# HGRN scan on one Trainium2 core: a level's four row multiplications made as two, with a stepped access pattern

## The chip, the core and the metric

One core of a Trainium2 chip runs the whole program. The metric is device microseconds of one execution; lower is better. Engines: TensorE (PE; its weight loads are listed as PEld), the Vector engine (DVE), ScalarE (ACT), GpSimd (POOL) and SyncE (SP).

## The reference, cut to what matters

One step of a two-layer diffusion backbone over 128 context and 512 latent tokens (T = 640 together). Each layer has one input projection, three bidirectional scans (SSD, HGRN2, mLSTM), a gated merge and a feed-forward part. The change is in the HGRN2 scan, four heads per layer, each in both directions:

```python
def hgrn_scan(q, k, v, logf, s0):
    causal = jnp.tril(jnp.ones((H_CHUNK, H_CHUNK), dtype=bool))[..., None]
    def step(s, inp):
        qc, kc, vc, gc = inp
        g = jnp.cumsum(gc, axis=-2)
        diff = jnp.where(causal, g[..., :, None, :] - g[..., None, :, :], 0.0)
        w = jnp.exp(diff) * causal
        att = jnp.einsum("bhtk,bhsk,bhtsk->bhts", qc, kc, w)
        o = jnp.einsum("bhts,bhsv->bhtv", att, vc) + jnp.einsum("bhtk,bhkv->bhtv", qc * jnp.exp(g), s)
        ...
```

A query at t and a key at s < t meet through the product of all forget gates f between them, channel by channel.

## The kernel before, in words

**Stages.** A layer runs bulk work on TensorE (projections of 128 rows by 640 tokens, with split weights: three matmuls of 320 columns for each half and each block of 128 inputs) and, woven into it, the scans. `drive` does this: a scan is a generator that yields numbers, and for each unit yielded one quantum of bulk work is emitted, which for a projection is six matmuls (`accumulate`, L485 to L494). TensorE's order is the order in which the code emits. Vector engine, ScalarE, SP and GpSimd are ordered by the build's scheduler, statically; each engine then works its own list in order, waiting on semaphores.

**A head of the HGRN scan** (`hgrn_scan`, L1258). The tile QK holds four sections of T columns: section 0 is q for the backward direction, 1 and 2 the keys k of forward and backward, 3 is q forward. Instead of a product over chunks, seven levels work on blocks of L = 1, 2, 4, ..., 64 tokens. At a level, pairs of neighbouring blocks of L meet: ScalarE copies the keys of both directions, a half of each pair of blocks from section 1 and the other half from section 2, into `hk` (L1293); TensorE multiplies them with the matching halves of sections 0 and 3 into the PSUM tiles `hl`, in two groups of three and two chunks of 128 (L1305); two COPY_PREDICATED put those scores that belong to this level into A (`hA`, L1323). Then the keys and queries must be carried to the block size 2L: half of the blocks of each section are multiplied by the product of the gates of the neighbouring block, which stands in the tile F (views `Fs[li]`, two sections of T/L values). These are the four multiplications of the change, L1316 to L1321, in the order of sections 1, 2, 0, 3. Below, sections 1 and 2 are the inner ones, 0 and 3 the outer ones. L1324 makes the next level's gate products.

So a level's `hk` needs the inner sections after the level before, and its `hl` needs `hk` and the outer sections. Between the `hl` of two levels the scan yields 3, which is 18 bulk matmuls.

**Beside it on the Vector engine**: the low parts of split weights (`wl`, L412), row products for the modulation (`jk`, `wa`, L289, with a small `mod`, L294). **On ScalarE**: the high parts of split weights (`wh`, L411) and copies of finished projections (`hq`, `mq`, `hth`, `val`, `bgt`). SP's queue issues the loads of weights.

Of the kernel before, what the change touches and what calls it, by code (L numbers as in the profile page):

```python
# [12 lines left out]
ALU = mybir.AluOpType  # L13
# [3 lines left out]
P = 128  # L17
# [4 lines left out]
T = CTX + SMP  # L22
# [86 lines left out]
def backbone(ctx, tc, a):  # L109
    nc = tc.nc  # L110
    pe, act, dve, pool_e = nc.tensor, nc.scalar, nc.vector, nc.gpsimd
# [16 lines left out]
    def ut(s, dt=F32):  # L128
        return up.tile([P, UW], dt, name=nm(s), tag="u")
# [4 lines left out]
    def bank(s):  # L134
        return ps.tile([P, 512], F32, name=nm(s), tag="ps")
# [612 lines left out]
    def mixers(i, h, ssum, spill, starter, spill_x, first_tickets):  # L748
# [5 lines left out]
        def qt(s):  # L754
            return qp.tile([P, 2560], F32, name=nm(s), tag="q")
# [482 lines left out]
        def halves_of(base, gap, L, nb):  # L1238
            return bass.AP(base.tensor, base.offset, [list(base.ap[0]), [2 * L, nb], [gap + L, 2], [1, L]])
# [18 lines left out]
        def hgrn_scan(u, hd):  # L1258
            q = u["q"]
            QK = qt("QK").rearrange("p (s f) -> p s f", s=4)  # L1260
# [10 lines left out]
            for d in range(2):  # L1271
# [3 lines left out]
                    out=f, in0=u[f"f{d}"][:, :T], scalar1=fsc[:, i, col], scalar2=fbi[:, i, col], op0=ALU.mult, op1=ALU.add  # L1275
# [14 lines left out]
            for li, L in enumerate(LEVELS):  # L1290
                nb = T // (2 * L)
                kk = ut("hk")
                act.activation(  # L1293
                    out=kk[:, :T].rearrange("p (b h j) -> p b h j", h=2, j=L), in_=halves_of(QK[:, 1, :], T, L, nb), func=AF.Copy
                )
                if li:
                    yield 3
                else:
                    yield 1
                copies = []  # L1300
                for c0, c1 in groups:
                    pt = bank("hl")
                    for c in range(c0, c1):
                        sl = slice(c * P, (c + 1) * P)
                        pe.matmul(  # L1305
                            pt[:, (c - c0) * P : (c - c0 + 1) * P], kk[:, sl], halves_of(QK[:, 0, sl], 3 * T, L, P // (2 * L)),
                            start=True, stop=True,
                        )
                    copies.append(dict(
                        out=A[:, c0 * P : c1 * P].rearrange("p (c f) -> p c f", f=P),  # L1310
                        mask=lmask[:, li, :].unsqueeze(1).to_broadcast([P, c1 - c0, P]),
                        data=pt[:, : (c1 - c0) * P].rearrange("p (c f) -> p c f", f=P),
                    ))
                fv = Fs[li].rearrange("p s (b h) -> p s b h", h=2)
                qv = QK.rearrange("p s (b h j) -> p s b h j", h=2, j=L)
                for s_ in (1, 2, 0, 3):  # L1316
                    half, s2 = s_ // 2, s_ % 2
                    dst = qv[:, s_, :, half, :]
                    dve.tensor_tensor(
                        out=dst, in0=dst, in1=fv[:, s2, :, 1 - half].unsqueeze(2).to_broadcast([P, nb, L]), op=ALU.mult,  # L1320
                    )  # L1321
                for cp in copies:
                    dve.copy_predicated(**cp)  # L1323
                dve.tensor_tensor(out=Fs[li + 1], in0=fv[:, :, :, 0], in1=fv[:, :, :, 1], op=ALU.mult)  # L1324
# [11 lines left out]
            for n in range(4):  # L1336
                pt = bank("hup")
                for d in range(2):
                    j = 2 * n + d
# [6 lines left out]
                for d in range(2):  # L1346
                    c = order[2 * n + d][1]
                    dve.scalar_tensor_tensor(
                        out=Sv[:, n, d, :], in0=Sv[:, n - 1, d, :], scalar=Fl[:, 1 - d, c : c + 1],
                        in1=pt[:, d * P : (d + 1) * P], op0=ALU.mult, op1=ALU.add,  # L1350
# [115 lines left out]
        def bg_item(f):  # L1466
# [7 lines left out]
            return item(f"bg{f}", O_BG + f * P, "bg", done)  # L1474

        kinds = (("S", ssd_items, sz_items, ssd_scan), ("H", hgrn_items, hg_item, hgrn_scan), ("M", mlstm_items, mo_item, mlstm_scan))
        of_kind = {k_: [{} for _ in range(4)] for k_ in "SHM"}
        units = [(k_, n, of_kind[k_][n]) + tuple(fs) for k_, *fs in kinds for n in range(4)]
# [162 lines left out]
    h, staged = modulator(0, x, 1, staged=True)  # L1641
# [141 lines left out]
    for i in range(DEPTH):  # L1783
# [13 lines left out]
        with tc.tile_pool(name=f"ff{i}", bufs=NF) as fp:  # L1797
# [37 lines left out]
            blocks, half, twin_blocks = block_modulator(i, x, fp)  # L1835
            h = [tuple(tuple(blocks[k][hf][:, m * HALF : (m + 1) * HALF] for hf in range(2)) for m in range(2)) for k in range(KT)]
# [4 lines left out]
            for n_, (p0, p1) in enumerate(PARTS):  # L1841
# [58 lines left out]
                if i + 1 < DEPTH:  # L1900
                    ada_need(i + 1, 15)
                    h, half = modulator(i + 1, x, 1)
                else:
                    half = final
# [107 lines left out]
```

## Time and profile before

| | |
|---|---|
| three runs | 2805.67, 2806.61, 2809.32 us, median 2806.61 |
| the profiled execution | 2810.28 us, of which the span of the trace is 2808.5 |
| TensorE, matmuls | 2755.0 us busy (98%) |
| Vector engine | 1914.2 us (68%), 3854 instructions |
| ScalarE | 1230.1 us (44%) |
| granted TensorE clock, mean | 0.993 of full |
| chain that ended last | TensorE 92%, Vector engine 3% |
| the four multiplications, L1319 | 224 of 128x320, 97.6 us busy |

Busy time of an engine is the time in which it had an instruction in work; on the Vector engine neighbouring instructions overlap by a little, so the sum of durations is larger than the busy time, and the time from start to start is shorter than a duration. In a timeline, a row's first number is its start in us from the start of the span, the second the time from the first start to the last end of the merged instructions, xN their number; a bracket gives idle time before it and what ended it.

### The profile page before, as it was taken

To read this page: it belongs to the slowest core of one execution; us is meant where nothing else is said; L and a number is where in the kernel's file an instruction comes from. 1 tells how busy PE (TensorE), PEld (TensorE's weight loads), DVE (VectorE), ACT (ScalarE), POOL (GpSimd) and SP (SyncE) were. 2 spreads that over 40 slices of the span, in tenths; PEclk is the share of its full clock that TensorE was granted. 3 is DMA by queue.
4 is the path that set the end of the run, shared out by engine and by line. 5 is a ranking of instruction groups with operands and counts; after the bars stand their busy time and mean duration, and the time that the engine had idled before them with its cause. 6 is when DMAs were issued, how large, how long until landed. Compare 5 with 4: busy or idle time off the path is not lost.

```text
span 2808.5 us, 48685 instructions
## 1 busy us (share of the span) xinstructions
PE 2755.0 (98%) x19262; PEld 2704.8 (96%) x19262; DVE 1914.2 (68%) x3854; ACT 1230.1 (44%) x2436; POOL 280.3 (10%) x474
## 2 busy tenths in 40 slices
PE   7999999999899999999999999999999999999998
PEld 6999999999899999999999999999999999999998
DVE  6657678777555586777777665888765556747475
ACT  5545434445442363342455544344445225425243
POOL 0111100000031100000001211000101200000000
PEclk9999999999999999999999999999999999999999
DMA  8444423434364324344534444333433733333433
GB/s 315 130 114 137 122 93 123 126 130 121 127 239 162 103 64 153 125 127 166 172 100 126 125 122 137 116 113 128 124 123 132 254 105 96 100 130 103 130 108 98
DMA packets 119300, 373.43 MB, mean 133 GB/s; under 512 B 16072, under 2 KB 28688, under 8 KB 118944
## 3 DMA queue, kind: packets, MB, share of 16 engines
q1 hardware_dynamic: 92720, 269.56, 30.7%
q0 software_dynamic: 26352, 100.76, 10.5%
q8 instruction: 152, 2.49, 0.4%
q14 instruction: 76, 0.62, 0.1%
HBM read 316.04 MB, written 54.21 MB: 132 GB/s over the span
## 4 chain that ended last, share of the span: by engine, by line
PE 92%; DVE 3%; DMA 2%; ACT 2%; issue 1%; SPq 0%; POOL 0%; ACTq 0%; DVEq 0%; POOLq 0%
PE ga L422 17%; PE ab L494 15%; PE bg L494 12%; PE br L494 8%; PE hfp L494 4%; PE sz L494 4%; PE xT L494 4%; PE hl L1305 2%; PE ga L494 2%; PE hgp L494 2%; PE hqp L494 2%; PE mkp L494 2%; PE BT L494 2%; PE CT L494 2%; PE mop L494 1%; PE val L1042 1%
## 5 line engine op out<-in xcount | busy, mean ns | idle before, releaser
L411 ACT ACTIVATE wh<-wr 128x1024 fp32r<-128x1024 f32 (+3 forms) x354 | 351.5, 996 | 569.0 <-PE br L494 144.1
L412 DVE TENSOR_TENSOR wl<-wr,wh 128x1024 fp32r<-128x1024 f32 (+3 forms) x354 | 407.7, 1153 | 191.2 <-ACT wh L411 186.6
L422 PE MATMUL ga<-hb,wh 128*128 128x320 f32 x912 | 201.6, 308 | 0.0
L1561 DVE SCALAR_TENSOR_TENSOR x<-ab,hg,x 128x128 f32<-128x128 f32 (+2 forms) x192 | 73.2, 433 | 170.3 <-PE ab L494 170.3
L494 PE MATMUL bg<-hh,wh 128*128 128x320 f32 x768 | 188.0, 326 | 0.0
L422 PE MATMUL ga<-hth,wl 128*128 128x320 f32 x608 | 187.8, 309 | 0.0
L422 PE MATMUL ga<-htl,wh 128*128 128x320 f32 x608 | 187.8, 309 | 0.0
L422 PE MATMUL ga<-hth,wh 128*128 128x320 f32 x608 | 187.7, 309 | 0.0
L494 PE MATMUL bg<-hl,wh 128*128 128x320 f32 x768 | 175.4, 310 | 0.0
L494 PE MATMUL bg<-hh,wl 128*128 128x320 f32 x768 | 175.2, 309 | 0.0
L494 PE MATMUL ab<-uh,wh 128*128 128x320 f32 x704 | 164.8, 310 | 0.0
L494 PE MATMUL ab<-ul,wh 128*128 128x320 f32 x704 | 164.1, 309 | 0.0
L494 PE MATMUL ab<-uh,wl 128*128 128x320 f32 x704 | 164.1, 309 | 0.0
L422 PEld LDWEIGHTS ga<-hb,wh 128*128 128x128 f32 x912 | 152.4, 188 | 0.0
L422 PE MATMUL ga<-hb,wl 128*128 128x320 f32 x456 | 140.6, 308 | 0.0
L494 PEld LDWEIGHTS bg<-hl,wh 128*128 128x128 f32 x768 | 129.3, 189 | 0.0
L494 PEld LDWEIGHTS bg<-hh,wh 128*128 128x128 f32 x768 | 127.0, 190 | 2.1 <-issue 0.8
L494 PEld LDWEIGHTS bg<-hh,wl 128*128 128x128 f32 x768 | 128.9, 189 | 0.0
L494 PEld LDWEIGHTS ab<-ul,wh 128*128 128x128 f32 x704 | 118.8, 188 | 0.2
L494 PEld LDWEIGHTS ab<-uh,wh 128*128 128x128 f32 x704 | 118.7, 188 | 0.2
L494 PEld LDWEIGHTS ab<-uh,wl 128*128 128x128 f32 x704 | 118.7, 188 | 0.0
L1153 ACT ACTIVATE E<-E,gsb 128x128 f32<-128x128 f32 x320 | 99.6, 392 | 37.3 <-POOL E L943 37.3
(497 smaller groups left out, 7552.7 us busy)
## 6 DMA issues: line engine op xcount, KB each, us to landing
wr<-w_in SPq DMA_DIRECT2D x152, 512.0 KB, 3.5
wr<-w_gu SPq DMA_DIRECT2D x88, 512.0 KB, 3.7
wa<-w_ada SPq DMA_DIRECT2D x84, 512.0 KB, 3.6
E<-rows_s SPq DMA_DIRECT2D x80, 256.0 KB, 5.8
x<-xd POOLq DMA_DIRECT2D x64, 320.0 KB, 3.7
wr<-w_down SPq DMA_DIRECT2D x32, 512.0 KB, 4.1
sp<-bgt POOLq DMA_DIRECT2D x48, 320.0 KB, 3.5
bgr<-sp POOLq DMA_DIRECT2D x48, 320.0 KB, 4.9
```

The source lines that it names most:

```text
L411: act.activation(out=hi[:, :n], in_=raw[:, :n], func=AF.Copy)
L412: dve.tensor_tensor(out=lo[:, :n], in0=raw[:, :n], in1=hi[:, :n].bitcast(F32), op=ALU.subtract)
L422: pe.matmul(bank_[:, :HALF], a_[:, sl], b_, start=first and j == m == 0, stop=j == n - 1 and m == 2, skip_group_check=True,)
L494: pe.matmul(out[hf][:, :HALF], wt_[:, sl], b_, start=m == k == 0, stop=m == 2 and k == n - 1)
L1042: pe.matmul(o, xh[:, sl], hi[:, wsl], start=k == 0, stop=False)
L1153: act.activation(out=e[:, j * P : (j + 1) * P], in_=e[:, j * P : (j + 1) * P], func=AF.Exp, bias=gv["sb"][:, d, c, 4 * g + j : 4 * g + j + 1],
L1305: pe.matmul(pt[:, (c - c0) * P : (c - c0 + 1) * P], kk[:, sl], halves_of(QK[:, 0, sl], 3 * T, L, P // (2 * L)), start=True, stop=True,)
L1561: dve.scalar_tensor_tensor(out=x_[:, lo:hi], in0=pt[:, lo - hf * HALF : hi - hf * HALF], scalar=gate[:, 2 * f + j : 2 * f + j + 1], in1=x_ ...
```

## The change

Per level, the multiplications of sections 1 and 2 become one operation over `2 x nb x L` elements (nb = T/2L), and those of 0 and 3 another. The access pattern of the destination steps from one section's blocks to the other's by T + L, or by 3T + L; that of the factor steps back or forward between the two sections of F.

```diff
                 fv = Fs[li].rearrange("p s (b h) -> p s b h", h=2)
-                qv = QK.rearrange("p s (b h j) -> p s b h j", h=2, j=L)
-                for s_ in (1, 2, 0, 3):
-                    half, s2 = s_ // 2, s_ % 2
-                    dst = qv[:, s_, :, half, :]
-                    dve.tensor_tensor(
-                        out=dst, in0=dst, in1=fv[:, s2, :, 1 - half].unsqueeze(2).to_broadcast([P, nb, L]), op=ALU.mult,
-                    )
+                for q0, step, f0, back in ((T, T + L, 2 * nb + 1, -2 * nb - 1), (0, 3 * T + L, 1, 2 * nb - 1)):
+                    dst = bass.AP(QK.tensor, QK.offset + q0, [list(QK.ap[0]), [step, 2], [2 * L, nb], [1, L]])
+                    by = bass.AP(fv.tensor, fv.offset + f0, [list(fv.ap[0]), [back, 2], [2, nb], [0, L]])
+                    dve.tensor_tensor(out=dst, in0=dst, in1=by, op=ALU.mult)
                 for cp in copies:
                     dve.copy_predicated(**cp)
```

TensorE's and GpSimd's orders stay as they were. On the Vector engine, ScalarE and SP instructions move, all within the HGRN stages. Names in the rows: out<-in with tile names, the size, and in brackets the engines' semaphores that the instruction waits for.

The Vector engine in the first head, level 2 (blocks of 4) and the start of level 3; before:

```order
L1319 TENSOR_TENSOR QK_4325<-QK_4325,F_4326 128x80x4 [waits Activation_49]
L1319 TENSOR_TENSOR QK_4325<-QK_4325,F_4326 128x80x4 [waits DVE_49]
L1319 TENSOR_TENSOR QK_4325<-QK_4325,F_4326 128x80x4 [waits DVE_49,PE_49]
L1319 TENSOR_TENSOR QK_4325<-QK_4325,F_4326 128x80x4 [waits DVE_49]
L1323 COPY_PREDICATED hA_4335<-lmask,hl_4477 128x384 [waits DVE_49]
L1323 COPY_PREDICATED hA_4335<-lmask,hl_4481 128x256 [waits DVE_49]
L1319 TENSOR_TENSOR QK_4325<-QK_4325,F_4326 128x40x8 [waits Activation_49]
```

and of the change, where L1318 is the merged multiplication and L1320 the predicated copy:

```order
L1320 COPY_PREDICATED hA_4335<-lmask,hl_4473 128x384 [waits DVE_49,PE_49]
L1318 TENSOR_TENSOR QK_4325<-QK_4325,F_4326 128x2x80x4 [waits PE_49,Activation_49]
L1320 COPY_PREDICATED hA_4335<-lmask,hl_4477 128x256 [waits DVE_49]
L1318 TENSOR_TENSOR QK_4325<-QK_4325,F_4326 128x2x80x4 [waits DVE_49]
L294 TENSOR_SCALAR mod_86<-mod_86,pv_84 128x2
L1320 COPY_PREDICATED hA_4335<-lmask,hl_4505 128x384 [waits PE_49]
L1318 TENSOR_TENSOR QK_4325<-QK_4325,F_4326 128x2x40x8 [waits PE_49,Activation_49]
```

The inner multiplication now waits for TensorE too, and stands behind the first predicated copy; the outer stands behind the second one, and waits for the inner.

TensorE at the products `hl` of the same level, with a bulk matmul on either side; before:

```order
L494 MATMUL hqp_4424<-hh_397,wl_4359 128x320
L1305 MATMUL hl_4477<-QK_4325,hk_4451 128x128 [waits DVE_49,PE_49,Activation_49]
L1305 MATMUL hl_4477<-QK_4325,hk_4451 128x128 x2
L1305 MATMUL hl_4481<-QK_4325,hk_4451 128x128 [waits PE_49]
L1305 MATMUL hl_4481<-QK_4325,hk_4451 128x128
L494 MATMUL hqp_4423<-hh_404,wh_4358 128x320
```

and of the change:

```order
L494 MATMUL hqp_4422<-hh_397,wl_4359 128x320
L1305 MATMUL hl_4473<-QK_4325,hk_4447 128x128 [waits PE_49,Activation_49]
L1305 MATMUL hl_4473<-QK_4325,hk_4447 128x128 x2
L1305 MATMUL hl_4477<-QK_4325,hk_4447 128x128 [waits PE_49]
L1305 MATMUL hl_4477<-QK_4325,hk_4447 128x128
L494 MATMUL hqp_4421<-hh_404,wh_4358 128x320
```

The place is the same; the wait for the Vector engine is gone from the first product, and in the built program the count for which ScalarE's `hk` waits is now that of the outer multiplication (it was that of the second inner one).

ScalarE in the second head, from the copy of level 0 to that of level 2; before:

```order
L1293 ACTIVATE hk_4997<-QK_4923 128x640 [waits DVE_49]
L1288 ACTIVATE hA_4933<-hd_4993 128x256 [waits PE_49]
L1293 ACTIVATE hk_5019<-QK_4923 128x640 [waits DVE_49]
L411 ACTIVATE wh_5342<-wr_5139 128x1024 [waits DMAHW2_49,PE_49]
L959 ACTIVATE hq_5033<-hqp_4946 128x320 [waits DMASW3_49,PE_49]
L959 ACTIVATE hq_5033<-hqp_4947 128x320 [waits PE_49]
L1293 ACTIVATE hk_5063<-QK_4923 128x640 [waits DVE_49]
```

and of the change:

```order
L1293 ACTIVATE hk_4983<-QK_4909 128x640 [waits DVE_49]
L1288 ACTIVATE hA_4919<-hd_4979 128x256 [waits PE_49]
L411 ACTIVATE wh_5314<-wr_5117 128x1024 [waits DMAHW2_49,PE_49]
L1293 ACTIVATE hk_5003<-QK_4909 128x640 [waits DVE_49]
L959 ACTIVATE hq_5017<-hqp_4932 128x320 [waits DMASW3_49,PE_49]
L959 ACTIVATE hq_5017<-hqp_4933 128x320 [waits PE_49]
L1293 ACTIVATE hk_5045<-QK_4909 128x640 [waits DVE_49]
```

The weight split `wh` has moved ahead of the copy of level 1; the fourth head has the same move.

## Rows read from the trace of the kernel before

**Rows 1.** Busy time by engine in the HGRN stages of both layers: us, busy (xcount), PEclk.

```profile
380.00:620.00 240.00, 239.31 (x1786) 237.52 (x1785) 195.90 (x423) 102.51 (x211) 11.88 (x22) 1.00 0.36 117
1760.00:2000.00 240.00, 239.22 (x1784) 237.12 (x1783) 201.18 (x432) 101.99 (x209) 11.87 (x22) 1.00 0.36 119
```

**Rows 2.** Line L1305: what ended the idle time before it (us, times).

```profile
  ACT hk L1293: 4.9, 16
```

**Rows 3.** Timeline of PEld, head 0: the loads of `hl`, levels 0, 1, 2, 4.

```profile
403.10 1.60 PEld L1305 LDWEIGHTS hl<-QK,hk 128*128 128x128 f32 x10 [0.43 <-ACT hk L1293]
407.52 1.26 PEld L1305 LDWEIGHTS hl<-QK,hk 128*128 128x128 f32 x10
411.32 1.23 PEld L1305 LDWEIGHTS hl<-QK,hk 128*128 128x128 f32 x10
...
418.86 1.23 PEld L1305 LDWEIGHTS hl<-QK,hk 128*128 128x128 f32 x10
```

**Rows 4.** The same for heads 1 (levels 0, 4, 5), 2 and 3 (levels 0, 4).

```profile
460.70 1.60 PEld L1305 LDWEIGHTS hl<-QK,hk 128*128 128x128 f32 x10 [0.44 <-ACT hk L1293]
...
474.66 1.20 PEld L1305 LDWEIGHTS hl<-QK,hk 128*128 128x128 f32 x10
477.90 1.20 PEld L1305 LDWEIGHTS hl<-QK,hk 128*128 128x128 f32 x10
...
520.06 1.60 PEld L1305 LDWEIGHTS hl<-QK,hk 128*128 128x128 f32 x10 [0.44 <-ACT hk L1293]
...
535.75 1.22 PEld L1305 LDWEIGHTS hl<-QK,hk 128*128 128x128 f32 x10
...
577.59 1.60 PEld L1305 LDWEIGHTS hl<-QK,hk 128*128 128x128 f32 x10 [0.43 <-ACT hk L1293]
...
592.87 1.20 PEld L1305 LDWEIGHTS hl<-QK,hk 128*128 128x128 f32 x10
```

**Rows 5.** Tile QK: its multiplications of 320 and 640 elements, ns min/median/max.

```profile
L1319 DVE TENSOR_TENSOR QK<-QK,F x224: 462/483/495, 405.1 to 1983.7; 128x320 f32<-128x320 f32 x112
...
L1278 DVE TENSOR_TENSOR QK<-hq,F x16: 815/818/821, 385.2 to 1945.7; 128x640 f32<-128x640 f32 x16
```

**Rows 6.** Timeline of the Vector engine: one of 640 elements and the next instruction.

```profile
385.19 0.82 DVE L1278 TENSOR_TENSOR QK<-hq,F 128x640 f32<-128x640 f32 x1
385.93 0.48 DVE L1199 TENSOR_TENSOR yt<-yt,ytr 128x128 f32<-128x128 f32 x2
```

**Rows 7.** Timelines of Vector engine and ScalarE, head 0, from level 0 to level 1.

```profile
405.10 1.70 DVE L1319 TENSOR_TENSOR QK<-QK,F 128x320 f32<-128x320 f32 x4
406.72 0.44 DVE L1323 COPY_PREDICATED hA<-lmask,hl 128x256 f32<-128x256 uint8 x1
407.05 1.21 DVE L412 TENSOR_TENSOR wl<-wr,wh 128x1024 fp32r<-128x1024 f32 x1
...
406.66 0.81 ACT L1293 ACTIVATE hk<-QK 128x640 f32<-128x640 f32 x1
```

**Rows 8.** The same two engines in head 0, levels 2 to 4.

```profile
411.74 0.89 DVE L1319 TENSOR_TENSOR QK<-QK,F 128x320 f32<-128x320 f32 x2
412.77 0.89 DVE L1319 TENSOR_TENSOR QK<-QK,F 128x320 f32<-128x320 f32 x2 [0.15 <-PE hl L1305]
...
416.34 0.60 DVE L1323 COPY_PREDICATED hA<-lmask,hl 128x384 f32<-128x384 uint8 x1
416.83 0.88 DVE L1319 TENSOR_TENSOR QK<-QK,F 128x320 f32<-128x320 f32 x2
...
412.71 0.74 ACT L1293 ACTIVATE hk<-QK 128x640 f32<-128x640 f32 x1 [1.73 <-DVE QK L1319]
```

**Rows 9.** Timeline of ScalarE, head 1: the weight split near level 1.

```profile
464.38 1.05 ACT L411 ACTIVATE wh<-wr 128x1024 fp32r<-128x1024 f32 x1
```

**Rows 10.** TensorE in the next scan: us, busy (xcount), PEclk, DMA share, GB/s.

```profile
705.00:710.00 5.00, 1.68 (x11) 1.00 0.70 266
710.00:715.00 5.00, 5.00 (x27) 0.66 0.00 0
```

## The prediction

> **What bounds the kernel now.** First the busy times of the two HGRN stages, by stretch [rows 1]: in 240 us TensorE works 239.3, in the second layer 239.2; the Vector engine works 196 and 201. So TensorE is the bound in both, and the Vector engine has a sixth of its time to spare. Second, what TensorE waited for before a level's product hl [rows 2]: 4.9 us over 16 waits in 56 levels. Eight of these are the first level of a head, 0.43 or 0.44 each, 3.5 in all [rows 3, 4]; the change does not touch them. What is left, 1.4 us, is all that shortening the multiplications can give back directly. Third, the pace of the levels, as the starts of TensorE's loads for hl [rows 3, 4]: TensorE does five products for hl, then 18 bulk matmuls of a projection, and the levels follow each other every 3.8 us in head 0 and every 3.2 us in head 1. So nothing of the scan holds TensorE today: the copy hk and the multiplications of a level run beside the bulk matmuls. The question is how much room they have there.
>
> **The change, part by part.** Names: level 0 to 6 of a head; "inner" are sections 1 and 2 of QK, which the next copy hk reads; "outer" are sections 0 and 3, which the products hl read.
>
> (a) Work of the Vector engine. 224 multiplications of 320 elements become 112 of 640: 0.483 and 0.818 us [rows 5]. Back to back, one is issued every 0.41 us (four in 1.70 [rows 7]), one of 640 every 0.74 (385.19 to 385.93 [rows 6]). Each merge frees 2 x 0.41 - 0.74 = 0.07 us, 112 of them 8 us. The row for 640 is of contiguous rows; the 320 ones already step through memory at every level, and all take 0.462 to 0.495, so I take no extra for the pattern. These 8 us lie beside TensorE's work [rows 1]; I cost them at nothing. Bounds: 0 to -1.4 us.
>
> The Trainium skill, "VectorE: DVE Perf Modes", section "Rules for kernel authors", says of chained operations to keep down their number, not the semaphores. By that rule the change is a gain, of the 8 us worked out in (a) at most. The trace says that the engine that would gain is not the one that bounds.
>
> (b) The order of the scan. A merged operation reaches over all that lies between its two rows: the inner pair over sections 1 and 2, the outer pair over 0 to 3, sections 1 and 2 included. The build orders accesses to QK by this reach, wherever it doesn't see that they are apart. So three waits come in, seen in the order above: at levels 0 to 3 the inner operation waits for the products hl of its own level (before: from level 2 on for hk alone); the outer waits for the inner; and the next copy hk waits for the outer. The last shows on TensorE: hl names no wait for the Vector engine any more, as hk has already waited for the later operation. Besides, one COPY_PREDICATED stands between inner and outer. Before, the inner operations of a level could run while TensorE was at hl, and hk of the next level began before or beside the outer ones. Now it is one chain: hl, inner, predicated copy, outer, hk, next hl.
>
> Its length, from the start of hl:
> - To the Vector engine's start after all five products: 405.10 - 403.10 = 2.00 us at level 0 [rows 3, 7], 412.77 - 411.32 = 1.45 later [rows 3, 8]. At levels 2 and 3 the first predicated copy fits in front.
> - Inner operation until the next is issued: 0.74 [rows 6].
> - Predicated copy: 406.72 to 407.05 = 0.33 for 256 columns [rows 7]; at level 1 the one of 384 stands there, 416.34 to 416.83 = 0.49 [rows 8].
> - Outer operation to its end: 0.82 [rows 5].
> - End of a multiplication to the start of hk: 411.74 + 0.89 to 412.71 = 0.08 [rows 8].
> - hk: 0.81 for level 1 [rows 7], 0.74 from level 2 [rows 8].
> - End of hk to the load for hl: 406.66 + 0.81 to 407.52 = 0.05 [rows 3, 7].
>
> Level 0 to 1: 2.00 + 0.74 + 0.33 + 0.82 + 0.08 + 0.81 + 0.05 = 4.83. Level 1 to 2: 1.45 + 0.74 + 0.49 + 0.82 + 0.08 + 0.74 + 0.05 = 4.37. Levels 2 to 3 and 3 to 4: with 0.33, 4.21 each. Together 17.62 us per head. Before, the same four steps took 15.76 in head 0, 13.96 in head 1, 15.69 in head 2, 15.28 in head 3 [rows 3, 4], 60.69 in all. Now 4 x 17.62 = 70.48: 9.8 us more per layer, 19.6 for both (the second layer is the same code, and its stretch has the same busy times [rows 1]).
>
> The last two steps cost nothing: from level 4 on the inner operation waits for hk alone and stands ahead of both predicated copies. The chain is 1.45 + 0.82 + 0.08 + 0.74 + 0.05 = 3.14, the pace 474.66 to 477.90 = 3.24 in the fastest head [rows 4]. That room is only 0.1 us; where it is gone, 16 steps cost perhaps 0.1 to 0.2 each. I keep 0 and leave 3 us to the range.
>
> (c) Other work on the Vector engine. Weight splits and ada products (1.2 us each) now stand behind the outer operation, before the next hl is through: from 3.3 us after hl to 4.21 + 1.45. They fit, but two of them only just. Cost 0; cover gone, it would be some tenths in the eight steps from level 0 to 1.
>
> (d) ScalarE. In heads 1 and 3 the split wh is moved ahead of hk for level 1. In the trace it runs from 464.38 to 465.43 [rows 9]; the new hk could begin at 460.70 + 2.00 + 0.74 + 0.33 + 0.82 + 0.08 = 464.67. If wh can't begin earlier than it did, hk is late by 0.76; if its weights and its buffer are free in time, by nothing. Between the two I take 0.3, nearer to nothing since what wh waits for on TensorE stands only ten bulk matmuls behind hl, for four heads 1.2 us. Other copies of ScalarE behind hk (hq, hth, val) come up to 1 us later; TensorE has two more pairs of banks, so I cost it at nothing.
>
> (e) SP's queue: some loads of weights and ada rows change places by a few positions. They are for weights needed at least one projection (48 matmuls) later; cost 0.
>
> Sum: 19.6 + 1.2 = 20.8 us, all of it waits of TensorE before hl, and in a stretch with no slack in it, so all of it arrives at the end. The profiled execution took 2810.28 (span 2808.5), so 2831.1; it stands 3.7 above the median of the three runs, 2806.61, and against that median I forecast **2827 us**. Bounds: if every one of the 32 steps is 0.2 us shorter, 14; if 0.2 longer and the last two steps stall, 30.
>
> **Rivals.**
> - *The waits are there, but hidden: no change.* It decides at a chain of about 3.8 us. That needs the 640 element operation to take about 0.48 instead of 0.82, issued every 0.41. Then the four steps are 4.16, 3.70, 3.54 and 3.54: nothing is lost in heads 0 and 2, about 1 us in head 1, 0.1 in head 3, and 2.2 us in two layers: 2809. For it: the order of the engines is unchanged but for a few places, and TensorE has bulk work between two levels. Against it: 16 rows of 640 elements, none below 0.815 [rows 5].
> - *The saving arrives: faster.* The 8 us of (a) come off the path, 2799. It needs TensorE to be waiting for the Vector engine in these stages, and it waits 1.4 us that the change could touch [rows 1, 2]. This is also where the page's rule leads.
> - *The clock goes too: slower still.* A pause of TensorE of 3.3 us in a stretch of the next scan was followed by 5 us at a granted clock of 0.66 instead of 1.00 [rows 10], a mean between the 1.2 and 2.4 GHz levels. That costs 5 x (1 / 0.66 - 1), about 2.6 us. If the waits of each of the eight heads brought one such stretch, 21 us more: 2848. Against it: the waits are 0.4 to 1.0 us each, with 3 us and more of work between, and the present waits of 0.44 leave 1.00 in the whole stage [rows 1].
>
> **How the numbers follow.** What a measurement of this kernel tells from no change is about 0.2%, 5.6 us. Forecast 0.80, hidden 0.12, saving 0.02, clock 0.06. Faster 0.02, same 0.12, slower 0.86. The range holds the forecast with its bounds (14 to 30 us over the median) and some way towards each neighbour: 2814 to 2841 us.
>
> **What would show it.** Right: TensorE waits for hk some 40 times, 25 us in all instead of 4.9; the first four steps of every head are 4.2 to 4.8 us apart in all heads alike, the last two as before; ScalarE's wait before hk for the multiplications grows above 76 us, and hk starts behind the outer operation, never beside it; 112 multiplications of about 0.82; the Vector engine's busy time falls by 6 to 8 us; outside the two stages nothing moves. Wrong: levels still 3.2 to 3.8 apart and no new waits before hl; multiplications well off 0.82; or a granted clock below 1.00 in the two stages.

## The result, and the profile after

The changed kernel takes **2830.77 us** (median of five runs, 2828.97 to 2833.08) against 2807.29 for the kernel before (five runs, 2805.67 to 2809.84): ratio 1.0083, 95% interval 1.0071 to 1.0095. It is 23.5 us slower; the forecast was 2827 us, with 2814 to 2841 as the range. The two profiled executions took 2810.28 and 2832.96 us; their spans are 2808.5 and 2830.9, 22.4 apart. Line numbers behind the change are smaller by up to three: the multiplications are L1318, the predicated copies L1320.

First the page of the changed kernel: busy time of each engine, and the chain that ended last.

```profile
PE 2762.5 (98%) x19262; PEld 2705.0 (96%) x19262; DVE 1906.4 (67%) x3742; ACT 1230.0 (43%) x2436; POOL 280.7 (10%) x474
...
PE 88%; DVE 6%; ACT 3%; DMA 1%; issue 1%; SPq 0%; POOL 0%; DVEq 0%; ACTq 0%; POOLq 0%
```

The Vector engine has 112 instructions fewer and is 7.8 us less busy (1914.2 before), as worked out. Its share of the chain has nevertheless doubled, from 3% to 6%, and ScalarE's went from 2% to 3%: what takes less time on its engine now stands in the way of the end. That is where to look for the loss, and not in the totals.

The same two stretches as in [rows 1] (us, busy time and number of PE, PEld, DVE, ACT, POOL, granted clock, DMA share, GB/s):

```profile
380.00:620.00 240.00, 232.40 (x1698) 226.93 (x1697) 187.90 (x356) 94.26 (x186) 8.63 (x16) 1.00 0.32 109
1760.00:2000.00 240.00, 232.44 (x1673) 225.73 (x1672) 188.72 (x356) 92.25 (x182) 8.11 (x15) 1.00 0.34 113
```

TensorE, which stood still for 0.7 and 0.8 us of the two stretches before, now does for 7.6 in each, and gets about 100 matmuls less done in the same 240 us. The granted clock is 1.00 in both (the 2.4 GHz level), as before.

What TensorE waited for ahead of the products hl, from the waits of PE and PEld (us in total, times, longest), answering to [rows 2]:

```profile
PE hl L1305 <- ACT hk L1293: 15.1, 40, 0.9
PEld hl L1305 <- ACT hk L1293: 25.0, 40, 1.1
```

Forty waits on each: eight heads with five levels each, the first level as before and four new ones. The two rows are the same waits seen twice, by the weight loads and by the matmuls, so they are not to be added; [rows 2] does add them (3.5 us in eight waits of loads and 1.4 in eight of matmuls make its 4.9 in 16). The loads' waits have grown by 21.5 us. The matmuls' waits are shorter, and TensorE's busy time is 7.5 us longer for the same 19262 matmuls (2755.0 before): so the loss is read from the loads. Where they are, the loads for hl show, heads 0 and 1, levels 0 to 6 (start, length, idle time before it):

```profile
404.65 1.60 PEld L1305 LDWEIGHTS hl<-QK,hk 128*128 128x128 f32 x10 [0.43 <-ACT hk L1293]
409.47 1.26 PEld L1305 LDWEIGHTS hl<-QK,hk 128*128 128x128 f32 x10 [0.56 <-ACT hk L1293]
413.90 1.19 PEld L1305 LDWEIGHTS hl<-QK,hk 128*128 128x128 f32 x10 [0.59 <-ACT hk L1293]
418.17 1.19 PEld L1305 LDWEIGHTS hl<-QK,hk 128*128 128x128 f32 x10 [0.50 <-ACT hk L1293]
422.38 1.19 PEld L1305 LDWEIGHTS hl<-QK,hk 128*128 128x128 f32 x10 [0.45 <-ACT hk L1293]
426.09 1.23 PEld L1305 LDWEIGHTS hl<-QK,hk 128*128 128x128 f32 x10
429.83 1.23 PEld L1305 LDWEIGHTS hl<-QK,hk 128*128 128x128 f32 x10
...
464.17 1.60 PEld L1305 LDWEIGHTS hl<-QK,hk 128*128 128x128 f32 x10 [0.44 <-ACT hk L1293]
469.42 1.26 PEld L1305 LDWEIGHTS hl<-QK,hk 128*128 128x128 f32 x10 [1.06 <-ACT hk L1293]
473.85 1.19 PEld L1305 LDWEIGHTS hl<-QK,hk 128*128 128x128 f32 x10 [1.04 <-ACT hk L1293]
478.05 1.19 PEld L1305 LDWEIGHTS hl<-QK,hk 128*128 128x128 f32 x10 [0.90 <-ACT hk L1293]
482.25 1.19 PEld L1305 LDWEIGHTS hl<-QK,hk 128*128 128x128 f32 x10 [0.92 <-ACT hk L1293]
485.50 1.20 PEld L1305 LDWEIGHTS hl<-QK,hk 128*128 128x128 f32 x10
```

Read the differences of the starts. The first four steps of head 0 are 4.82, 4.43, 4.27 and 4.21, of head 1 5.25, 4.43, 4.20 and 4.20: the two heads, which differed by 1.8 us before [rows 3, 4], now go at almost one pace. This is the mark of a chain that doesn't care how long the bulk matmuls between two levels take. The steps behind level 4 are 3.7 and 3.25, as before, with no wait. From level 0 to 4, the eight heads of both layers took 121.37 us before and take 143.19 now: 21.8 of the 22.4 us between the spans. From level 4 to 6 they took 55.87 and take 55.80.

The links of that chain, as the Vector engine and ScalarE show them from level 2 to 3 of head 0 (hl starts at 413.90 and 418.17):

```profile
414.88 0.59 DVE L1320 COPY_PREDICATED hA<-lmask,hl 128x384 f32<-128x384 uint8 x1 [0.32 <-PE hl L1305]
415.40 0.82 DVE L1318 TENSOR_TENSOR QK<-QK,F 128x640 f32<-128x640 f32 x1
416.14 0.44 DVE L1320 COPY_PREDICATED hA<-lmask,hl 128x256 f32<-128x256 uint8 x1
416.47 0.82 DVE L1318 TENSOR_TENSOR QK<-QK,F 128x640 f32<-128x640 f32 x1
...
417.38 0.74 ACT L1293 ACTIVATE hk<-QK 128x640 f32<-128x640 f32 x1 [3.53 <-DVE QK L1318]
```

Products, inner multiplication at 415.40, predicated copy, outer multiplication until 417.29, and only then hk, at 417.38; its end, 418.12, releases hl. Before, hk of that step ran from 412.71 to 413.45 [rows 8], while hl, with no wait, began only here:

```profile
415.10 1.23 PEld L1305 LDWEIGHTS hl<-QK,hk 128*128 128x128 f32 x10
```

It had 1.6 us to spare, and has none now.

The multiplications themselves, on the tile QK (ns min/median/max), and ScalarE's wait for them:

```profile
L1318 DVE TENSOR_TENSOR QK<-QK,F x112: 802/818/833, 406.6 to 2007.0; 128x640 f32<-128x640 f32 x112
...
  ACT hk L1293: 105.7, 43
```

0.818 us in the median, to the nanosecond that of the contiguous rows in [rows 5]. The last row is what ScalarE's hk waited for them in all: 105.7 us in 43 waits (76.0 before).

### The profile page after: what moved, and what is told of

Same layout as the page of the kernel before. It is cut to its first block, busy times and chain, and to the rows that moved or that the text cites. A ratio compares the mean times of both kernels' runs of the same rounds, so it can differ in the third digit from the quotient of the medians.

```text
span 2830.9 us, 48539 instructions
## 1 busy us (share of the span) xinstructions
PE 2762.5 (98%) x19262; PEld 2705.0 (96%) x19262; DVE 1906.4 (67%) x3742; ACT 1230.0 (43%) x2436; POOL 280.7 (10%) x474
## 4 chain that ended last, share of the span: by engine, by line
PE 88%; DVE 6%; ACT 3%; DMA 1%; issue 1%; SPq 0%; POOL 0%; DVEq 0%; ACTq 0%; POOLq 0%
PE ga L422 16%; PE ab L494 14%; PE bg L494 11%; PE br L494 8%; PE sz L494 4%; PE xT L494 4%; PE hfp L494 4%; PE ga L494 2%; PE hl L1305 2%; PE BT L494 2%; PE hgp L494 2%; PE CT L494 2%; DVE QK L1318 2%; PE mop L494 1%; PE mkp L494 1%; PE pi L1178 1%
```

## The experiments

The theory: the loss is made of waits, and the waits come from the reach of a merged operation, that is, from all the memory between its first and its last element, which the build orders against other accesses even where the operation doesn't touch it. The rivals: the merged operations are slow in themselves (pattern or length); or the loss lies in something else that moved. Each run below has a run of the kernel before beside it on the same chip (medians 2808.08 for the first four, 2807.71 for the last two). The diffs are cut to the lines that count and stand against the kernel before.

**One pair merged at a time.** First the inner sections alone; the outer ones stay two operations:

```diff
+                for q0, step, f0, back in ((T, T + L, 2 * nb + 1, -2 * nb - 1),):
+                    dst = bass.AP(QK.tensor, QK.offset + q0, [list(QK.ap[0]), [step, 2], [2 * L, nb], [1, L]])
...
-                for s_ in (1, 2, 0, 3):
+                for s_ in (0, 3):
```

> Only the inner pair (sections 1 and 2) is merged; the outer rows stay two operations of 320. Theory (what costs is that the next copy hk waits behind the outer operation): hk waits for the inner operation alone, and the chain from one hl to the next is 1.45 + 0.82 + 0.08 + 0.74 + 0.05 = 3.14 us (3.76 from level 0), less than the pace of any head; no new waits of TensorE, 2807 us, within 2 us of before; levels 3.2 to 3.8 apart. Rival (an operation of 640 is itself too long for the scan, or merging as such shifts the engines' orders): half of the loss is seen, about 2818 us.

Measured: 2808.33 us, ratio 0.9998 (0.9989 to 1.0007). No loss that can be told. Head 0 of this run, level 1, shows why (Vector engine, then ScalarE; here L1318 is the merged operation, L1323 the two single ones):

```profile
409.47 0.82 DVE L1318 TENSOR_TENSOR QK<-QK,F 128x640 f32<-128x640 f32 x1
410.21 0.89 DVE L1323 TENSOR_TENSOR QK<-QK,F 128x320 f32<-128x320 f32 x2
...
410.33 0.74 ACT L1293 ACTIVATE hk<-QK 128x640 f32<-128x640 f32 x1 [2.00 <-DVE QK L1318]
```

The copy hk starts 0.04 us after the merged operation ends (410.29), beside the outer multiplications. The inner operation's own wait for hl is there, but the pace of the levels has room for it, nearly: four waits of 0.17 to 0.27 us behind the first level are new, in the fast heads 1 and 3, where none was expected. They are 0.9 us in all.

Then the outer sections alone:

```diff
-                for s_ in (1, 2, 0, 3):
+                for s_ in (1, 2):
...
+                for q0, step, f0, back in ((0, 3 * T + L, 1, 2 * nb - 1),):
```

> Only the outer pair (sections 0 and 3) is merged; the inner rows stay two operations of 320. Theory: the outer operation reaches over the inner sections, so hk waits for it; at levels 0 and 1 the inner two also wait for hl, so the steps are about 2.00 + 0.41 + 0.41 + 0.33 + 0.82 + 0.94 = 4.9 and 1.45 + 0.82 + 0.49 + 0.82 + 0.87 = 4.45 us; from level 2 on the inner two run beside hl and the step is 3.2 us, below the pace. TensorE waits at two steps of each head, 12 to 14 us over eight heads: 2819 to 2821 us, half or more of the loss. Rival (each merged operation costs the same by its length): the same as with the inner pair merged alone.

Measured: 2819.31 us, ratio 1.0036 (1.0023 to 1.0050): half of the loss, from half of the merging. Loads for hl in head 0, levels 0 to 4:

```profile
405.02 1.60 PEld L1305 LDWEIGHTS hl<-QK,hk 128*128 128x128 f32 x10 [0.43 <-ACT hk L1293]
409.91 1.26 PEld L1305 LDWEIGHTS hl<-QK,hk 128*128 128x128 f32 x10 [0.63 <-ACT hk L1293]
414.42 1.19 PEld L1305 LDWEIGHTS hl<-QK,hk 128*128 128x128 f32 x10 [0.66 <-ACT hk L1293]
418.17 1.23 PEld L1305 LDWEIGHTS hl<-QK,hk 128*128 128x128 f32 x10
421.93 1.23 PEld L1305 LDWEIGHTS hl<-QK,hk 128*128 128x128 f32 x10
```

Two steps of 4.89 and 4.51, and two of 3.75 and 3.76 as in the kernel before. The wait of hk for the outer operation is there at every level of this head; here at level 3, where it costs nothing (L1325 is the merged operation):

```profile
419.66 0.81 DVE L1325 TENSOR_TENSOR QK<-QK,F 128x640 f32<-128x640 f32 x1
...
420.50 0.74 ACT L1293 ACTIVATE hk<-QK 128x640 f32<-128x640 f32 x1 [1.23 <-DVE QK L1325]
```

At levels 0 and 1 it makes the chain too long, by 0.07 more than in the changed kernel, as two inner operations take 0.82 and the merged one 0.74. From level 2 on the inner operations, alone, no longer wait for hl, and the chain fits again. Over all eight heads the first two steps are 12.7 us longer than before (11.9 in the changed kernel), the next two 0.9 (9.9 in the changed kernel). So the two parts don't add up (0 and 11 make 23): it is the inner operation's wait for hl together with the outer one's hold on hk that closes the chain at levels 2 and 3.

**The reach without the merging.** Four operations of about 320 elements again, but each with a half of the blocks of both sections, so that each reaches from the one section into the other as a merged one does:

```diff
+                for q0, step, f0, back in ((T, T + L, 2 * nb + 1, -2 * nb - 1), (0, 3 * T + L, 1, 2 * nb - 1)):
+                    for b0, b1 in ((0, (nb + 1) // 2), ((nb + 1) // 2, nb)):
...
+                        dve.tensor_tensor(out=dst, in0=dst, in1=by, op=ALU.mult)
```

> Nothing is merged in number: four operations per level of about 320 elements as before, but each takes half of the blocks of both sections of a pair, so that each has the reach of the merged ones. Theory: hk waits behind all four, and other work (weight splits, ada products of 1.2 us) stands between some of them on the Vector engine; steps of about 5.1 to 6.2, 5.8 to 6.2 and 4.4 us at levels 0, 1 and 2, and the old pace from level 3 on; a loss of about 35 us, 2842 us (2830 to 2850), without any longer operation. Rival (the length of the merged operation): as before, 2807 us.

Measured: 2849.14 us (2846.20 to 2851.94), ratio 1.0145 (1.0131 to 1.0158): slower than the merged kernel, with operations as short as those before. So the length of a merged operation is not the cause: the long reach loses time without it. TensorE's idle time before hl, loads and matmuls added (40.1 us in 80 waits in the changed kernel):

```profile
  ACT hk L1293: 66.1, 62
```

The plainest step is the one from level 2 to 3 of head 0, where nothing but one predicated copy stands among the four multiplications on the Vector engine:

```profile
417.55 0.89 DVE L1319 TENSOR_TENSOR QK<-QK,F 128x320 f32<-128x320 f32 x2
418.36 0.44 DVE L1321 COPY_PREDICATED hA<-lmask,hl 128x256 f32<-128x256 uint8 x1
418.69 0.88 DVE L1319 TENSOR_TENSOR QK<-QK,F 128x320 f32<-128x320 f32 x2
420.44 0.89 DVE L1319 TENSOR_TENSOR QK<-QK,F 128x320 f32<-128x320 f32 x2 [0.87 <-ACT hk L1293]
...
419.67 0.74 ACT L1293 ACTIVATE hk<-QK 128x640 f32<-128x640 f32 x1 [3.66 <-DVE QK L1319]
```

hk starts 0.10 us after the last of the four ends, and the step takes 4.40 us (3.78 before, 4.27 in the changed kernel). The row at 420.44 is the inner pair of level 3: it starts 0.02 us before that level's first load for hl, waits for hk alone, and from there the old pace is back (3.73), though it reaches from the one section into the other as the merged operation does, which waits there. So the reach counts where the build doesn't see that two patterns are apart; by what rule it sees that, no run here tells.

That this kernel is slower than the merged one comes from the first two steps. The Vector engine's row at level 0 of head 0, and ScalarE's hk behind it:

```profile
406.85 1.01 DVE L1319 TENSOR_TENSOR QK<-QK,F 128x320 f32<-128x320 f32 x2
407.78 1.23 DVE L412 TENSOR_TENSOR wl<-wr,wh 128x1024 fp32r<-128x1024 f32 x1
408.93 0.48 DVE L1319 TENSOR_TENSOR QK<-QK,F 128x320 f32<-128x320 f32 x1
...
409.45 0.85 ACT L1293 ACTIVATE hk<-QK 128x640 f32<-128x640 f32 x1 [1.70 <-DVE QK L1319]
```

The build's scheduler puts a weight split of 1.15 us between the two outer halves, and hk waits for the last half. This step takes 6.2 us (4.8 in the changed kernel), and the steps from level 1 to 2 have the like (5.7 to 6.1 us). All of this was in the expectation, and the steps bear it out: they are 36.8 us longer than before in the eight heads, where about 35 were worked out. The medians are 41.1 apart. Of the four executions two took 2846 us, the profiled one among them, and two 2851 to 2852; where the latter lost their 5 us no trace shows.

**The sections apart.** Now both pairs merged as in the change, but with the keys in sections 0 and 1 and the queries in 2 and 3, so that no merged operation reaches over the other pair. Every multiplication, copy and product is the same; only its place in QK differs:

```diff
-                dve.tensor_scalar(out=QK[:, 1 + d, :], in0=f, scalar1=-1.0, scalar2=1.0, op0=ALU.mult, op1=ALU.add)
-                dve.tensor_tensor(out=QK[:, 3 * (1 - d), :], in0=q[:, :T], in1=f, op=ALU.mult)
+                dve.tensor_scalar(out=QK[:, d, :], in0=f, scalar1=-1.0, scalar2=1.0, op0=ALU.mult, op1=ALU.add)
+                dve.tensor_tensor(out=QK[:, 3 - d, :], in0=q[:, :T], in1=f, op=ALU.mult)
...
-                            pt[:, (c - c0) * P : (c - c0 + 1) * P], kk[:, sl], halves_of(QK[:, 0, sl], 3 * T, L, P // (2 * L)),
+                            pt[:, (c - c0) * P : (c - c0 + 1) * P], kk[:, sl], halves_of(QK[:, 2, sl], T, L, P // (2 * L)),
...
+                for q0, step, f0, back in ((0, T + L, 2 * nb + 1, -2 * nb - 1), (2 * T, T + L, 1, 2 * nb - 1)):
```

The other readers of QK (the copy hk, the key sums, the transposes, the last products) take the new places too. One reach besides that of the outer operation becomes shorter by this, that of hl: its operand stepped from section 0 to section 3, over the inner ones, by 3T, in the change and in the kernel before alike, and now steps by T between the two queries.

> Both pairs merged as in the change, with the sections of QK in another order: the two inner ones in the first half of the tile, the two outer ones in the second, so that neither operation reaches over the other pair. The same 112 operations of 640 with steps in their patterns. Theory: no wait is left that the arithmetic doesn't need; hk waits for the inner operation, which doesn't wait for hl even at levels 0 and 1. The loss is gone: 2806 us, at most 1.4 us below before (the waits of TensorE before hl that are not the first of a head), 2805 to 2808; Vector engine busy 6 to 8 us less than before. Rival (the longer stepped operation is the cause): the loss stays, 2828 to 2832 us.

Measured: 2806.51 us, ratio 0.9990 (0.9981 to 0.9999). The 23 us are gone, with 112 merged operations of the same length. Whether the rest is a gain was left to a second timing of the same program, beside a kernel with the new places and the four single multiplications:

```diff
-                    dst = qv[:, s_, :, half, :]
+                    dst = qv[:, (2, 0, 1, 3)[s_], :, half, :]
```

> The sections stand as in the run with the sections apart (keys at 0 and 1, queries at 2 and 3), but the four multiplications stay four operations of 320. Theory of the reach: every one of the four reaches over its own section alone, as in the kernel before, so no wait comes in and none goes; the layout by itself changes nothing: ratio to before 0.9985 to 1.0010 (2804 to 2811 us), multiplications 224 of 0.48 us, Vector engine busy about 1914 us. Rival, that the new order of the sections is what gained, for instance because hk and hl read other places: then this kernel shares the gain of the merged one, 0.998 to 0.9985 or less, and the same two-level lead of hk over hl.

> The same program as the first run with the sections apart, timed again beside the kernel with the layout alone, to settle whether 2806.5 against 2808.1 is a gain. Theory: with the sections apart the merged operations bring no wait, and the 8 us that the Vector engine is spared lie beside TensorE's work, so the ratio to before is 1.000 within 0.001. Rival, that the saved 8 us arrive: they would give 2800, a ratio of 0.997. A ratio near 0.999 again, with an interval clear of 1, would be a small gain of some 2 us from the waits of TensorE in the HGRN stages, which cannot be more than 1.4 us by the row for the waits before hl.

Measured: 2806.33 us for the places alone, ratio 0.9992 (0.9983 to 1.0001), and 2806.45 for merging and places, ratio 0.9993 (0.9984 to 1.0001). Neither can be told from the kernel before, nor from the other. Busy times of the two, places alone first:

```profile
PE 2751.3 (98%) x19262; PEld 2700.8 (96%) x19262; DVE 1913.8 (68%) x3854; ACT 1231.2 (44%) x2436; POOL 279.1 (10%) x474
```

```profile
PE 2750.8 (98%) x19262; PEld 2701.7 (96%) x19262; DVE 1906.7 (68%) x3742; ACT 1230.4 (44%) x2436; POOL 277.6 (10%) x474
```

The merging saves its 7.1 us on the Vector engine; the medians differ by 0.1 us, the other way, and each interval is some 2.5 us wide to either side. This is the change without its waits, and it is worth nothing here that can be told. The merged one's rows in head 0 show how much room there is (Vector engine, ScalarE, loads for hl at levels 0 and 1):

```profile
403.92 0.83 DVE L1318 TENSOR_TENSOR QK<-QK,F 128x640 f32<-128x640 f32 x1 [2.02 <-ACT hk L1293]
```

```profile
404.79 0.82 ACT L1293 ACTIVATE hk<-QK 128x640 f32<-128x640 f32 x1 [0.62 <-DVE QK L1318]
```

```profile
403.94 1.60 PEld L1305 LDWEIGHTS hl<-QK,hk 128*128 128x128 f32 x10 [0.43 <-ACT hk L1293]
408.17 1.30 PEld L1305 LDWEIGHTS hl<-QK,hk 128*128 128x128 f32 x10
```

The inner multiplication starts 0.02 us before the first load for hl instead of 2.0 after it, and hk for level 1 ends at 405.61, 2.56 us before its hl.

So the theory needs a correction for one of the two waits. The outer operation does reach over the sections that hk reads, and hk waits for it. The inner operation stays within sections 1 and 2; what lies across it is hl's operand. This is why the inner multiplications waited for hl at levels 0 and 1 in the kernel before too, single as they were [rows 3, 7]; merging them carried that wait on to levels 2 and 3. The layout takes away both reaches at once, and no run here parts them.

## Why the prediction was right

It was right in its sign, in its size and in its mechanism; two terms were a little small, and one row was misread without harm.

*(a) The multiplications.* Right. 112 of 0.818 us, the Vector engine 7.8 us less busy where 8 were worked out, and nothing of it in the time. The runs with the sections apart test this alone, and find no difference. The misread row is [rows 2]: the 1.4 us of waits that I left as open to the change aren't. They are the matmuls' side of the eight waits at the first level of the heads, whose loads waited 3.5. The merged kernel with the sections apart shows the same 4.9 us over 16 waits, eight on PEld and eight on PE. There was nothing at all to give back. The sign "25 us in all instead of 4.9" has the same fault: by the view that gave 4.9, the changed kernel has 40.1 us over 80 waits; the 25.0 over 40 are the loads alone, and stand against 3.5 over 8.

The Trainium skill, "VectorE: DVE Perf Modes", section "Rules for kernel authors", tells to keep down the number of chained operations rather than the semaphores. The trace agrees for the Vector engine's busy time, which fell by 7.8 us (1914.2 to 1906.4). For the time of this kernel the number of operations decided nothing (2806.45 against 2806.33 us with the sections apart), and the waits that came with the smaller number cost 23.5 us.

*(b) The order of the scan.* Right, link by link. Predicted steps of a head: 4.83, 4.37, 4.21, 4.21; measured in head 0: 4.82, 4.43, 4.27, 4.21. The term that was mis-sized is the second step. The products hl of level 1 took longer than I read off level 2 of the kernel before, as TensorE's rows of the changed kernel show for the two levels (start, length), with the Vector engine's inner operation of level 1 below:

```profile
409.48 1.47 PE L1305 MATMUL hl<-QK,hk 128*128 128x128 f32 x10 [0.30 <-ACT hk L1293]
413.91 1.38 PE L1305 MATMUL hl<-QK,hk 128*128 128x128 f32 x10 [0.33 <-ACT hk L1293]
...
411.05 0.83 DVE L1318 TENSOR_TENSOR QK<-QK,F 128x640 f32<-128x640 f32 x1 [0.24 <-PE hl L1305]
```

The Vector engine started at 411.05, 1.58 us after the first load, and not after 1.45; other links were a little shorter, and what is left of this in the step, 0.06 us in eight heads, is 0.5 us. The last two steps cost nothing, as taken (55.80 against 55.87 us). Two of the three waits were shown apart by the runs: merging the inner pair alone costs nothing that can be told, the hold of the outer one on hk costs 11 us alone, the two together 23; with the sections apart there is none of it. The wait of the outer operation for the inner one was not tried by itself. That the inner operation waits for hl by hl's reach and not by its own, the prediction does not say.

*(c) Weight splits and ada products.* Right for this kernel: they fit behind the outer operation, and cost nothing. The run with four halves shows what this cover was worth, steps of 5.7 to 6.2 us where one of them got in between.

*(d) ScalarE's wh ahead of hk.* 0.3 us was taken, between 0 and 0.76. Measured is 0.40, in the rows of head 1 of the changed kernel:

```profile
467.26 0.82 DVE L1318 TENSOR_TENSOR QK<-QK,F 128x640 f32<-128x640 f32 x1
...
467.59 1.06 ACT L411 ACTIVATE wh<-wr 128x1024 fp32r<-128x1024 f32 x1 [3.20 <-PE hqp L494]
468.56 0.80 ACT L1293 ACTIVATE hk<-QK 128x640 f32<-128x640 f32 x1
```

By its chain hk could start at 467.26 + 0.82 + 0.08 = 468.16; it starts at 468.56, when wh, which waited for a bulk matmul, lets it. In four heads this is 0.4 us more than was put down.

*The sum.* 20.8 us were forecast, 21.8 are in the steps, 22.4 between the spans and 23.5 between the medians. The 1.0 us between the first two is the two terms above, 0.5 and 0.4. That steps and spans agree to 0.6 us is partly luck: in the other profiles the two, each against the kernel before, differ by up to 6.7 us (the first run with the sections apart: steps 0.7 shorter, span 7.4 shorter), and the first hl alone started anywhere from 401.2 to 405.6 us in the eight profiles of this study. No run shows where the rest between the steps and the medians went.

*The rivals.* The waits are not hidden: for that the 640 element operation had to take 0.48 us. The saving does not arrive, in either layout. The clock does not go: waits of up to 1.1 us left the granted clock at 1.00 in both stages.

## What to carry to other kernels

Before two operations are merged, look at the memory that lies between their two parts, and between the parts of what their neighbours read, not only at what they touch: the build here ordered by reach wherever it didn't see patterns apart, so the merged operations brought waits that the arithmetic doesn't need, and a slack of 1.6 us (level 3 of head 0) turned into a wait of 0.5. The cure was not to split them again but to put together in memory what is merged (2806.45 against 2830.77 us for the same operations). And the 7 us that such a merge spared were worth nothing here, as its engine didn't set the end: read the waits of the engine that bounds first, level by level; if none of them names the engine that would be spared, no gain is to be expected. Count a wait once, too: here the loads and the matmuls of TensorE each listed the same one.

## What had not been expected of the hardware

A stepped pattern of two sections of 640 values, with blocks from 1 to 64 long and the factor held or stepped backwards, took 0.802 to 0.833 us over all levels, the same as 640 contiguous values (0.812 to 0.820 in the same profile). Here the pattern itself was free.

Waits of TensorE's loads of 0.4 to 1.1 us at five levels of each head, with bulk work in between, left its granted clock at 1.00 in both stages. In the run with four halves single waits reached 2.7 us, and the stretches from 380 to 620 and from 1760 to 2000 us still had 1.00 and 0.99.
